# A one-layer hybrid encoder kernel: queries projected with the weights stationary and x^T moving, rotary embedding on rows packed through DRAM, pooling maps and one set of key transposes placed elsewhere

## The chip, the core and the metric

One Trainium2 chip, of which one core is used. The metric is the device time of one execution in microseconds (us), median of several runs. Engines are named as the profile names them: PE (TensorE, matmuls; PEld are its weight loads), DVE (VectorE), ACT (ScalarE), POOL (GpSimd) and SP (SyncE, which here only issues DMAs; ACT issues a few too). Each engine works through its own queue in order.

## The reference, cut to what is computed

```python
D_MODEL, SEQ, N_HEADS, D_LATENT = 1024, 2048, 8, 128      # one layer, batch 1
proj = x @ w_in        # columns: q 1024 | c_kv 128 | q_idx 512 | w_idx 8 | k_idx 64 | pool_in 512 | gates 2048
q = apply_partial_rope(q.reshape(B, S, N_HEADS, D_LATENT), cos_q, sin_q)   # first 32 of 128 dims: two halves of 16
k_lat = apply_partial_rope(c_kv, cos_q, sin_q)
q_idx, k_idx = ...     # rotated in the same way, 16 of 64 dims
attn = sparse_indexed_attention(q, k_lat, c_kv, q_idx, w_idx, k_idx)   # each query keeps its 256 best keys
attn = jnp.einsum('bshd,hde->bshe', attn, w_uv).reshape(B, S, ATTN_WIDTH)
branch_a = attn @ w_attn_branch
branch_b = multiscale_pool(pool_in, w_pool, pool_scale) @ w_pool_branch  # trailing means minus token, a 128x128 map per group
gate_a, gate_b = jnp.split(jax.nn.sigmoid(gate_logits), 2, axis=-1)
mixed = (gate_a * branch_a + gate_b * branch_b) @ w_out
x = layer_norm(ALPHA * x + mixed); x = layer_norm(ALPHA * x + conv_ffn(x))

def apply_partial_rope(x, cos, sin):     # half = 16 for q
    x1, x2 = x[..., :half], x[..., half:2 * half]
    return jnp.concatenate([x1 * cos - x2 * sin, x2 * cos + x1 * sin, x[..., 2 * half:]], axis=-1)
```

## The kernel before

Every float32 operand of a projection is split into a high and a low part (`split`, L312: on POOL in pieces of 256 columns, or on ACT for the high and DVE for the low part), and each product is three matmuls (`mm3`, L337). The 2048 tokens are worked in four groups of 512 (`G`), each of four row blocks of 128 (`RB`).

`run` (L1839) goes through these stages: for each group `proj_index` (indexer, keys and values; tokens in the rows of the result) and `finish_index` (rotary embedding of those rows); then for each group `proj_pool`, `proj_q` and `proj_gates`; then attention, the output projection and the feed-forward part. The steps that follow are in the second loop.

`proj_r` (L523) makes a product with tokens in rows: the stationary operand is a 128x128 piece of x^T, the moving one 256 columns of the weights. `proj_t` (L513) makes it transposed: the stationary operand is a 128x128 piece of the weights, the moving one 512 tokens of x^T. The pools and gates go by `proj_t`, the queries by `proj_r`. So `proj_q` (L648) computes, for four weight chunks of 256 columns (two heads), four row blocks of 24 matmuls of 256 columns each; ACT copies each result out; DVE rotates the rows (four products and two sums of 128x128 elements per chunk, `rope`, L534); and two chunks later `store_q` (L672) transposes them back on PE, 128x128 at a time (eight transposes per chunk, 32 per group), since attention wants q as (dim, head, token). ACT copies the transposed heads out and issues their store to `d_q`. `load_q` (L1064) fetches them, 128 tokens at a time, in attention.

Where `store_q` is called: from `proj_q` once more than two chunks are pending, and at the first two chunks of `proj_gates`. At the fourth gate chunk stand the four pooling maps (`pool_map`, L752; three matmuls each with `wpool`, their results taken out by ACT and DVE). The transposes of the last group's keys (`keys`, called through `done()`, L1869) stand after the second step of the first group's `proj_pool`.

What sets the order: the code is written as generators that yield between pieces of PE work. At each yield `turn` (L359) runs what was put off for some turns (`after`), issues the stores put off with `store` (SP, two turns later), and then, as a set of modelled clocks allows, takes steps from a background list: the indexer's scores (matmuls with `kst`) and a 32-step bisection for each query's 256th score (tiles `F`, `g`, `h`, `wd`, `wa`: counts on DVE and ACT over whole rows, each with a throw-away output from the pool of small tiles). That pool (`M`) has 8 buffers, the pool of large tiles (`T`) 42, and PSUM four banks of 512 columns (`PS1`) for the projections. Weights are fetched two chunks ahead and split one chunk ahead (`Weights.get`, L250), in group 0 from `w_in`, where the split parts are also stored (`wp`), and in later groups from those stored parts.

## Time and profile before

| | us |
|---|---|
| median of three runs | 3289.72 (3289.57 to 3299.82) |
| the profiled execution, its own time | 3292.94 |
| its span, first to last instruction | 3291.2 |
| PE busy in the span | 3157.8 (96%) |
| DVE, ACT, POOL busy | 2417.7 (73%), 1559.4 (47%), 1279.9 (39%) |
| mean granted clock of PE | 0.982 of 2.4 GHz |

In this trace the first loop ends at about 196 us with the first pooling matmuls; the keys' transposes of the last group begin at 201.8, group 0 of the second loop ends at 428.8, and the first matmul of attention starts at 1099.8. Nearly every operation is recorded by one helper and so has the line L153; rows are told apart by tiles and shapes. In tile names p is PSUM, b a large and m a small tile. A window of the trace gives, per engine, its busy time and in brackets the instructions in it, then PEclk, the granted clock as a share of 2.4 GHz, the DMA engines' busy share and GB/s.

### The profile page before, as it was taken

The numbers are of one execution on the slowest core, as the hardware profiler recorded it, in microseconds if no ns is written. First come the engines' busy times: TensorE is split into PE (matmuls) and PEld (weight loads), VectorE is DVE, ScalarE is ACT, GpSimd is POOL, SyncE is SP. The second block draws the span as 40 slices with busy tenths as digits, with TensorE's granted clock in tenths as the row PEclk, the third lists the DMA queues.
The fourth block names the chain that finished last, engine by engine and source line by source line (L and its number), as shares of the span: only waits on it lengthen the run. The fifth ranks groups of instructions, "written<-read, shape, count | busy, mean of one in ns | idle before, by whom it ended". The sixth has DMA issues, their size and how long they took to land. (4 is left out here: it accounts for less than half of the span.)

```text
span 3291.2 us, 46503 instructions
## 1 busy us (share of the span) xinstructions
PE 3157.8 (96%) x15918; PEld 2654.2 (81%) x15918; DVE 2417.7 (73%) x4271; ACT 1559.4 (47%) x2656; POOL 1279.9 (39%) x1314
## 2 busy tenths in 40 slices
PE   8988899999999899999999999999999999999998
PEld 8877688898898788788878877777778778888787
DVE  5588859986988777777766666666688865555797
ACT  3466537846777466666621133333343433222443
POOL 3139411020010688766641143443166511121673
PEclk9999899999999899999999999999999999999999
DMA  8457565653665444434464459899797665566984
GB/s 327 148 199 275 191 251 195 246 203 136 227 226 194 144 172 172 157 130 161 157 224 147 156 186 320 309 327 339 288 380 264 208 252 224 224 238 246 364 296 163
DMA packets 325675, 745.68 MB, mean 227 GB/s; under 512 B 30074, under 2 KB 115006, under 8 KB 325438
## 3 DMA queue, kind: packets, MB, share of 16 engines
q1 hardware_dynamic: 315646, 724.88, 61.5%
q10 hardware_dynamic: 9792, 17.83, 1.4%
q8 instruction: 126, 2.06, 0.3%
q14 instruction: 111, 0.91, 0.1%
HBM read 514.36 MB, written 228.23 MB: 226 GB/s over the span
## 5 line engine op out<-in xcount | busy, mean ns | idle before, releaser
L153 PE MATMUL p<-b,b 128*128 128x512 f32 (+3 forms) x12644 | 2783.7, 369 | 56.1 <-ACT b L153 24.4
L153 PEld LDWEIGHTS p<-b,b 128*128 128x128 f32 x12644 | 2175.7, 191 | 453.0 <-ACT b L153 25.0
L153 ACT ACTIVATE b<-p 128x512 fp32r<-128x512 f32 (+9 forms) x726 | 427.7, 612 | 653.6 <-PE p L153 627.0
L153 ACT ACTIVATE b<-b 128x1024 fp32r<-128x1024 f32 (+2 forms) x248 | 253.6, 1028 | 390.7 <-POOL b L153 136.4
L153 DVE TENSOR_TENSOR b<-b,b 128x1024 fp32r<-128x1024 f32 (+6 forms) x246 | 369.6, 1541 | 42.6 <-ACT b L153 39.8
L153 ACT ACTIVATE m<-b,F 128x1024 bf16<-128x1024 f32 (+3 forms) x352 | 345.8, 985 | 68.0 <-DVE F L153 43.8
L153 DVE TENSOR_SCALAR_CACHE_REDUCE m<-b,F 128x768 bf16<-128x768 f32 (+4 forms) x374 | 346.8, 949 | 11.8 <-DMA q<-m 9.9
L153 POOL TENSOR_TENSOR b<-b,b 128x256 fp32r<-128x256 f32 (+3 forms) x276 | 314.1, 1152 | 101.7 <-ACT b L153 84.9
L153 DVE TENSOR_TENSOR m<-m,p 128x512 f32<-128x512 f32 x176 | 120.3, 684 | 242.8 <-ACT b L153 182.6
L153 POOL TENSOR_TENSOR m<-b,b 128x512 f32<-128x512 f32 x99 | 140.2, 1425 | 337.4 <-issue 258.6
L153 DVE SCALAR_TENSOR_TENSOR b<-b,cw,b 128x1023 f32<-128x1023 f32 (+1 forms) x176 | 245.0, 1392 | 26.2 <-ACT b L153 25.1
L153 DVE TENSOR_TENSOR b<-p,b 128x512 fp32r<-128x512 f32 (+1 forms) x286 | 201.7, 714 | 72.3 <-ACT b L153 69.7
L153 POOL TENSOR_SCALAR b<-b 128x256 fp32r<-128x256 f32 (+3 forms) x216 | 125.8, 596 | 325.6 <-DMA b<-in_w_in_dram 122.8
L153 PE MATMUL p<-b 128*128 128x512 f32 x616 | 235.1, 393 | 5.8 <-ACT b L153 4.0
L153 POOL TENSOR_TENSOR b<-b,m 128x512 f32<-128x512 f32 x110 | 192.0, 1760 | 123.8 <-DMA m<-in_w_ffn_down_dram 74.0
L153 PE MATMUL p<-ident,b 128*128 128x128 f32 x1456 | 213.1, 274 | 24.8 <-ACT b L153 13.5
L153 DVE CUSTOM_DVE_ANT_0 b<-p,b 128x1024 f32<-128x1024 f32 (+7 forms) x192 | 174.2, 909 | 65.8 <-PE p L153 64.5
L153 PEld LDWEIGHTS p<-ident,b 128*128 128x128 f32 x1456 | 174.2, 141 | 58.7 <-ACT b L153 16.5
L153 ACT ACTIVATE b<-b,mx 128x1024 f32<-128x1024 f32 (+7 forms) x192 | 171.5, 896 | 69.7 <-DVE mx L153 63.7
L153 ACT ACTIVATE m<-p 128x512 f32<-128x512 f32 (+1 forms) x180 | 104.9, 594 | 193.6 <-PE p L153 178.9
L153 DVE SCALAR_TENSOR_TENSOR b<-b,ws,b 128x768 f32<-128x768 f32 (+5 forms) x154 | 159.8, 1065 | 40.6 <-ACT b L153 38.6
L153 PE MATMUL p<-kst,b 128*128 128x384 f32 (+3 forms) x656 | 150.6, 359 | 4.1 <-ACT b L153 2.6
(130 smaller groups left out, 2360.8 us busy)
## 6 DMA issues: line engine op xcount, KB each, us to landing
b<-uw SPq DMA_DIRECT2D x308, 512.0 KB, 6.5
b<-wp SPq DMA_DIRECT2D x192, 512.0 KB, 5.8
uw<-l SPq DMA_DIRECT2D x98, 512.0 KB, 3.0
b<-in_w_ffn_down_dram SPq DMA_DIRECT2D x154, 256.0 KB, 5.3
b<-h SPq DMA_DIRECT2D x154, 256.0 KB, 5.3
wp<-b SPq DMA_DIRECT2D x64, 512.0 KB, 5.2
uw<-b SPq DMA_DIRECT2D x56, 512.0 KB, 3.5
h<-m SPq DMA_DIRECT2D x110, 256.0 KB, 5.9
```

The lines of the kernel that those rows point to most:

```text
L153: return f(*args, **kw)
```

## The change

The queries go by `proj_t`: for each head one unit of 24 matmuls with 512 moving columns, whose result is already (dim, token). ACT copies it to a small tile `t` two turns later and stores dims 32 to 127 to `d_q`; SP stores the two halves of 16 rotary dims to `d_qx`, so that 8 heads x 16 dims fill 128 rows. At the second gate chunk these are loaded (`rope_load`), and during the third DVE rotates them with six operations of 128x512 (`rope_turn`) and stores them to `d_qr`; `load_q` fetches q in three pieces. The tables of cosines and sines come in the same packing: POOL widens them, PE transposes them (eight transposes per group) and ACT copies them out, in the first loop. `store_q` is gone. Of the splits that went to POOL, every fourth of all splits counted in the first two loops now goes to ACT and DVE. The four pooling maps stand between the units of the gates, one after each of units 4 to 7. The last keys' transposes stand four steps later.

```diff
+KEYS_AT = 5
+PM_AT = (4, 5, 6, 7)
...
     def split(self, hi, lo, src, pool=False):
-        if pool:
+        self.turns += 1
+        if pool and (not self.shared or self.turns % 4):
...
     def proj_index(self, g, done):
+            if c == 1:
+                self.rope_wide(g)
+            if c == 2:
+                self.rope_tables(g)
...
+    def rope_wide(self, g):
+        self.wide = []
+        for tab in (self.cos, self.sin):
+            t = self.M([P, RB, H, ROT])
+            self.nc.gpsimd.tensor_copy(t, tab[:, g * RB:(g + 1) * RB, None, :].to_broadcast([P, RB, H, ROT]))
+            self.wide.append(t)
+    def rope_tables(self, g):
+        nc = self.nc
+        for i, wide in enumerate(self.wide):
+            ps = self.PS1()
+            for rb in range(RB):
+                nc.tensor.transpose(ps[:, rb * P:(rb + 1) * P], wide[:, rb].rearrange("p h r -> p (h r)"), self.ident)
+            t = self.M([P, G])
+            nc.scalar.activation(t, ps, AF.Copy)
+            self.store(self.d_cs[g][:, i], t)
     def proj_q(self, g):
...
         for c in range(4):
             w = self.ab.get(base + c)
+            for i in range(2):
                 ps = self.PS1()
+                yield from self.proj_t(ps, w, i * P)
+                def keep(ps=ps, h=2 * c + i):
+                    t = self.M([P, G])
+                    nc.scalar.activation(t, ps, AF.Copy)
+                    nc.scalar.dma_start(self.d_q[g][2 * ROT:, h], t[2 * ROT:])
+                    for s in range(2):
+                        nc.sync.dma_start(self.d_qx[g][s][h * ROT:(h + 1) * ROT], t[s * ROT:(s + 1) * ROT])
+                self.after(DG, keep)
+                for _ in range(2):
                     self.lazy_step()
+                yield 5.2
+    def rope_load(self, g):
+        self.cs, self.qx = self.T([P, 2, G]), self.T([P, 2, G])
+        self.nc.sync.dma_start(self.cs, self.d_cs[g])
+        for s in range(2):
+            self.nc.sync.dma_start(self.qx[:, s], self.d_qx[g][s])
+    def rope_turn(self, g):
+        nc = self.nc
+        x, c, o = self.qx, self.cs, self.T([P, 2, G])
+        m = {}
+        def half(i, j, op):
+            def mul():
+                nc.vector.tensor_tensor(o[:, i], x[:, i], c[:, 0], op=OP.mult)
+            def cross():
+                m[i] = self.M([P, G])
+                nc.vector.tensor_tensor(m[i], x[:, j], c[:, 1], op=OP.mult)
+            def add():
+                nc.vector.tensor_tensor(o[:, i], o[:, i], m[i], op=op)
+                self.store(self.d_qr[g][i], o[:, i])
+            return [mul, cross, add]
+        return half(0, 1, OP.subtract) + half(1, 0, OP.add)
     def proj_gates(self, g):
...
-            if j == 3:
-                yield from self.pool_map(g)
-            if self.qpend and j < 2:
-                self.store_q()
+            if j == 1:
+                self.rope_load(g)
             while self.lazy or j and self.fins:
                 self.lazy_step()
+            if j == 2:
+                turning = self.rope_turn(g)
             for i in range(2):
                 ps = self.PS1()
-                yield from self.proj_t(ps, w, i * P)
+                for step in self.proj_t(ps, w, i * P):
+                    if j == 2:
+                        turning.pop(0)()
+                    yield step
...
-                yield 5.2
+                if 2 * j + i + 1 in PM_AT:
+                    yield 2.6
+                    self.pool_map(len(self.pm))
+                yield 2.6
...
     def load_q(self, b):
         q = self.T([P, H, P])
-        nc.sync.dma_start(q, self.d_q[g][:, :, rb * P:(rb + 1) * P])
+        cs = slice(rb * P, (rb + 1) * P)
+        nc.sync.dma_start(q[2 * ROT:], self.d_q[g][2 * ROT:, :, cs])
+        for s in range(2):
+            nc.sync.dma_start(q[s * ROT:(s + 1) * ROT], self.d_qr[g][s][:, cs].rearrange("(h r) c -> r h c", h=H))
...
             for i, step in enumerate(self.proj_pool(g)):
-                if i == 1 and g == 0:
+                if i == KEYS_AT and g == 0:
                     done()
```

Three places in the order of instructions. The first is PE in group 0, at the first pair of heads that `store_q` transposes. In the names p is a PSUM tile and b an SBUF tile, with the numbers of the program; `ident` is the identity of a transpose. Before:

```order
L153 MATMUL p_929_3797<-b_3420,b_2862 128x256
L153 MATMUL p_929_3797<-b_3420,b_2861 128x256
L153 MATMUL p_929_3797<-b_3421,b_2861 128x256
L153 MATMUL p_929_3797<-b_3420,b_2862 128x256
L153 MATMUL p_942_3850<-ident_84,b_3208 128x128 x4
L153 MATMUL p_944_3858<-ident_84,b_3208 128x128 x4
L153 MATMUL p_957_3895<-b_3629,b_2210 128x256
L153 MATMUL p_957_3895<-b_3630,b_2210 128x256
```

Now, between two units of the queries:

```order
L155 MATMUL p_830_3290<-b_2953,b_3132 128x512
L155 MATMUL p_830_3290<-b_2954,b_3132 128x512
L155 MATMUL p_830_3290<-b_2953,b_3133 128x512
L155 MATMUL p_853_3363<-b_2284,b_3122 128x512
L155 MATMUL p_853_3363<-b_2285,b_3122 128x512
L155 MATMUL p_853_3363<-b_2284,b_3123 128x512
```

The transposes are gone from PE's queue there, and one unit of 512 columns stands where two of 256 stood. Over the whole program PE has 15054 matmuls where it had 15918: 1536 of 256 columns are replaced by 768 of 512, 128 transposes are gone and 32 are added.

The second place is PE in group 0 at the pooling maps (tile `wpool`). Before, the four stand together between two units of the gates:

```order
L153 MATMUL p_1140_4540<-b_2861,b_4299 128x512
L153 MATMUL p_1168_4631<-b_3338,wpool_586 128x512 x3
L153 MATMUL p_1171_4641<-b_3516,wpool_586 128x512 x3
L153 MATMUL p_1178_4662<-b_3745,wpool_586 128x512 x3
L153 MATMUL p_1180_4669<-b_4032,wpool_586 128x512 x3
L153 MATMUL p_1184_4681<-b_2210,b_4459 128x512
```

Now the first of them, with a whole unit of 24 matmuls before it and one behind it:

```order
L155 MATMUL p_1098_4160<-b_2953,b_3927 128x512
L155 MATMUL p_1098_4160<-b_2954,b_3927 128x512
L155 MATMUL p_1098_4160<-b_2953,b_3928 128x512
L155 MATMUL p_1114_4221<-b_3347,wpool_606 128x512 x3
L155 MATMUL p_1128_4254<-b_2284,b_4069 128x512
L155 MATMUL p_1128_4254<-b_2285,b_4069 128x512
```

Each map has moved to a place of its own, 24 matmuls from the next.

The third place is SP in group 0's queries, between the stores of split weights (`wp`) and the fetches of later ones (`in_w_in_dram`). Before:

```order
L366 DMA wp_3432<-b_3194 128x1024
L366 DMA wp_3433<-b_3195 128x1024
L366 DMA wp_3649<-b_3410 128x1024
L212 DMA b_3625<-in_w_in_dram 128x4x256
L212 DMA b_3627<-in_w_in_dram 128x4x256
```

Now:

```order
L369 DMA wp_3288<-b_3132 128x1024
L369 DMA wp_3289<-b_3133 128x1024
L688 DMA qr_157<-m_3370 16x512
L688 DMA qr_158<-m_3370 16x512
L369 DMA wp_3457<-b_3272 128x1024
L369 DMA wp_3458<-b_3273 128x1024
L214 DMA b_3439<-in_w_in_dram 128x4x256
L214 DMA b_3441<-in_w_in_dram 128x4x256
```

Two stores of 16 rows from ACT's tile now stand in SP's queue for every head (64 in all), ahead of a later chunk's fetch; SP has 124 DMAs more.

## Rows read from the trace of the kernel before

**Rows 1.** The page's head, the busy time of each engine.

```profile
span 3291.2 us, 46503 instructions
PE 3157.8 (96%) x15918; PEld 2654.2 (81%) x15918; DVE 2417.7 (73%) x4271; ACT 1559.4 (47%) x2656; POOL 1279.9 (39%) x1314
```

**Rows 2.** Windows: group 0 of the second loop, the next part up to the end of group 1's queries, the rest of the second loop, and the start of attention.

```profile
201.80:428.80 227.00, 193.51 (x989) 164.62 (x988) 201.85 (x536) 128.47 (x250) 145.15 (x256) 0.90 0.69 245
428.80:560.00 131.20, 123.16 (x777) 110.45 (x776) 98.16 (x181) 78.81 (x141) 18.20 (x18) 0.97 0.50 186
560.00:1078.00 518.00, 515.52 (x2698) 444.46 (x2697) 441.33 (x1086) 366.65 (x673) 30.51 (x39) 1.00 0.59 211
1078.00:1131.00 53.00, 46.85 (x212) 38.23 (x211) 43.76 (x112) 22.84 (x59) 35.86 (x46) 0.84 0.45 143
```

**Rows 3.** PE's timeline in group 3, at the end of the queries and in the gates: start, duration and number of matmuls that follow each other in one shape.

```profile
971.24 1.04 PE L153 MATMUL p<-ident,b 128*128 128x128 f32 x8
972.04 11.75 PE L153 MATMUL p<-b,b 128*128 128x256 f32 x96
983.62 1.47 PE L153 MATMUL p<-ident,b 128*128 128x128 f32 x12
987.44 0.66 PE L153 MATMUL p<-ident,b 128*128 128x128 f32 x4 [2.35 <-ACT b L153]
...
1024.52 71.13 PE L153 MATMUL p<-b,b 128*128 128x512 f32 x313
```

**Rows 4.** The shapes on PE in group 0 (201.8 to 428.8), with the idle time before each and what ended it.

```profile
L153 PE MATMUL p<-b,b 128*128 128x512 f32 x553 | 132.4, 402 | 4.1 <-DVE b L153 3.4 <-ACT m L153 0.7
L153 PE MATMUL p<-b,b 128*128 128x256 f32 x384 | 49.8, 294 | 2.4 <-ACT b L153 2.4
L153 PE MATMUL p<-ident,b 128*128 128x128 f32 x32 | 5.3, 306 | 6.9 <-ACT b L153 6.9
L153 PE MATMUL p<-b,wpool 128*128 128x512 f32 x12 | 5.1, 550 | 9.8 <-ACT m L153 9.8
L153 PE MATMUL p<-ident,m 128*128 128x128 f32 x8 | 3.2, 412 | 10.2 <-DVE m L153 10.2
```

**Rows 5.** Windows inside group 0: the keys and the pools, the queries, the gates up to the maps, the maps.

```profile
201.80:232.90 31.10, 20.89 (x81) 15.89 (x80) 27.79 (x91) 16.53 (x31) 15.87 (x36) 0.78 0.64 227
232.90:295.40 62.50, 53.18 (x410) 52.03 (x408) 60.57 (x164) 43.64 (x93) 49.46 (x85) 0.93 0.66 229
295.40:332.30 36.90, 36.16 (x155) 29.61 (x154) 29.46 (x68) 21.18 (x40) 33.96 (x63) 0.94 0.95 349
332.30:350.60 18.30, 5.11 (x13) 2.51 (x12) 16.77 (x46) 13.77 (x28) 12.72 (x24) 0.65 0.76 232
```

**Rows 6.** The costliest small operations and the rotary operations on DVE in group 0: number, busy time, mean ns of one, idle time before.

```profile
L153 DVE SCALAR_TENSOR_TENSOR g<-wd,wa 128x4 f32<-128x4 f32 x32 | 16.7, 522 | 7.6 <-ACT m L153 6.9
L153 DVE TENSOR_SCALAR h<-g 128x4 int32<-128x4 f32 x32 | 10.8, 339 | 1.0
L153 DVE TENSOR_SCALAR h<-g 128x2 int32<-128x2 f32 x31 | 10.1, 325 | 1.0
L153 DVE SCALAR_TENSOR_TENSOR g<-wd,wa 128x2 f32<-128x2 f32 x31 | 9.2, 295 | 2.2 <-ACT m L153 1.8
L153 DVE SCALAR_TENSOR_TENSOR F<-h,F 128x4 int32<-128x4 int32 x31 | 8.7, 280 | 1.0
L153 DVE SCALAR_TENSOR_TENSOR F<-h,F 128x2 int32<-128x2 int32 x31 | 8.1, 261 | 1.0
L153 DVE TENSOR_TENSOR rope<-b,sin 128x128 f32<-128x128 f32 x8 | 4.5, 559 | 0.0
L153 DVE TENSOR_TENSOR rope<-b,cos 128x128 f32<-128x128 f32 x8 | 3.9, 492 | 0.0
L153 DVE TENSOR_TENSOR b<-rope,rope 128x128 f32<-128x128 f32 x8 | 3.7, 501 | 0.0
```

**Rows 7.** The same small operations on DVE from 570 to 680 us, a stretch of the second loop in which POOL is nearly idle.

```profile
L153 DVE TENSOR_SCALAR h<-g 128x2 int32<-128x2 f32 x46 | 7.8, 169 | 1.3
L153 DVE SCALAR_TENSOR_TENSOR g<-cd,ca 128x2 f32<-128x2 f32 x46 | 7.2, 157 | 4.6 <-ACT m L153 3.6
L153 DVE SCALAR_TENSOR_TENSOR F<-h,F 128x2 int32<-128x2 int32 x45 | 7.2, 160 | 1.4
```

**Rows 8.** The splits on POOL in group 0 (pieces of 256 columns, two operations each), and operations of the second loop (0 to 1131 us) on DVE that are like those that the change adds.

```profile
L153 POOL TENSOR_TENSOR b<-b,b 128x256 fp32r<-128x256 f32 x114 | 85.1, 767 | 0.0
L153 POOL TENSOR_SCALAR b<-b 128x256 fp32r<-128x256 f32 x114 | 50.3, 459 | 10.4 <-DMA b<-in_w_in_dram 6.7 <-DMA b<-in_w_pool_branch_dram 3.6
...
L153 DVE TENSOR_TENSOR b<-b,b 128x1024 fp32r<-128x1024 f32 x20 | 25.0, 1270 | 12.8 <-ACT b L153 12.3 <-DMA xT<-b 0.3
L153 DVE TENSOR_TENSOR b<-m,b 128x512 fp32r<-128x512 f32 x16 | 11.9, 745 | 0.7 <-ACT b L153 0.7
```

**Rows 9.** Waits of PE in group 1's queries and gates (530 to 572 us): in total, times, longest.

```profile
PE p L153 <- ACT b L153: 4.6, 2, 2.7
```

**Rows 10.** Waits for DMAs from 201.8 to 1131 us that end an idle time of DVE or ACT, and the two longest of SP's own queue from 428.8 to 1131 us.

```profile
DVE m L153 <- DMA q<-m: 9.9, 4, 3.1
ACT m L153 <- DMA q<-m: 6.4, 3, 3.4
DVE m L153 <- DMA gm<-m: 1.1, 1, 1.1
ACT m L153 <- DMA gm<-m: 1.0, 1, 1.0
...
SPq L220 <- DVE b L153: 131.2, 19, 29.4
SPq L220 <- PE p L153: 106.5, 39, 23.8
```

More of the change, by code (lines that the diff above doesn't have):

```diff
@@ L451, in setup @@
         self.d_q = [self.DT([P, H, G], name="q") for _ in range(NG)]
+        self.d_qx, self.d_qr = ([[self.DT([P, G], name="qr") for _ in range(2)] for _ in range(NG)] for _ in range(2))
+        self.d_cs = [self.DT([P, 2, G], name="cs") for _ in range(NG)]
         self.d_gm = [self.DT([P, DC, 2, G], name="gm") for _ in range(NG)]
@@ L650, in proj_q @@
         base = g * self.nab + 2
-        bs = slice(g * RB, (g + 1) * RB)
         for c in range(4):
             w = self.ab.get(base + c)
-            rows = self.T([P, RB, 256])
-            for rb in range(RB):
+            for i in range(2):
                 ps = self.PS1()
-                yield from self.proj_r(ps[:, :256], w, rb, 256)
-                self.after(DQ, lambda rb=rb, ps=ps, rows=rows:
-                           nc.scalar.activation(rows[:, rb], ps[:, :256], AF.Copy))
-                if rb:
-                    self.lazy_step()
-                yield 2.6
-            self.flush()
-            v = rows.rearrange("p b (h d) -> p b h d", d=DL)
-            cs, sn = (t[:, bs, None, :].to_broadcast([P, RB, 2, ROT]) for t in (self.cos, self.sin))
-            halves = (v[:, :, :, 0:16], v[:, :, :, 16:32])
-            self.rope(halves, halves, cs, sn, [P, RB, 2, ROT])
-            self.qpend.append((g, c, rows))
-            if len(self.qpend) > 2:
-                self.store_q()
@@ L672, in store_q @@
-    def store_q(self):
-        g, c, rows = self.qpend.pop(0)
-        for i in range(2):
-            ps = self.PS1()
-            for rb in range(RB):
-                self.nc.tensor.transpose(ps[:, rb * P:(rb + 1) * P], rows[:, rb, i * DL:(i + 1) * DL], self.ident)
-            t = self.M([P, G])
-            self.nc.scalar.activation(t, ps, AF.Copy)
-            self.nc.scalar.dma_start(self.d_q[g][:, 2 * c + i], t)
+                yield from self.proj_t(ps, w, i * P)
[5 more added lines that the diff above has]
+                        nc.sync.dma_start(self.d_qx[g][s][h * ROT:(h + 1) * ROT], t[s * ROT:(s + 1) * ROT])
@@ L750, in lazy_step, with pool_map @@
             self.lazy.pop(0)()
[L752 removed]
+    def pool_map(self, k):
         nc = self.nc
[L754 to L764 removed]
+        t = self.pooled[k]
+        ps = self.PS1()
+        self.mm3(ps, self.wpool[:, 0, k], self.wpool[:, 1, k], t[:, 0], t[:, 1], True, True)
+        o = self.T([P, 2, G], F32R)
+        sc = self.pscale[:, k:k + 1]
+        nc.scalar.activation(o[:, 0], ps, AF.Identity, scale=sc)
+        nc.vector.scalar_tensor_tensor(o[:, 1], ps, sc, o[:, 0].bitcast(F32), op0=OP.mult, op1=OP.subtract)
+        self.pm.append(o)
     def proj_gates(self, g):
```

23 lines of the change are left out of this document (7 added, 16 removed).

## The prediction

> **What bounds the kernel now.** I read the page's head first: PE is busy for 96% of the span, no other engine for over 73% [rows 1]. So the end is set by PE's work plus the time in which PE waits or runs at the lower of its two clocks. The change touches the second loop (196 to 1100 us), so I next read that loop in windows [rows 2]. From 560 to 1078 us PE is busy for 515.5 of 518 us at full clock (2.4 GHz): there a matmul less is time less. Group 0 is different: in 227.0 us PE's granted clock is 0.90 on average, and DVE is busy for 201.9 us. The matmuls' own need there follows from the counts [rows 4] and the spacing at full clock [rows 3]. Spacing is read from starts, since durations overlap: 96 matmuls of 256 columns go from 972.04 to 983.62, 120.6 ns each; 313 of 512 columns take 71.13 us, 227 ns each; eight transposes go from 971.24 to 972.04, 100 ns each. So 565 x 0.227 + 384 x 0.1206 + 40 x 0.1 = 178.6 us, and group 0 loses 48.4 us. The idle times in rows 4 say where: 10.2 us at the keys' transposes (waiting for DVE's rotations), 9.8 at the pooling maps, 9.3 in the queries and at their transposes, 4.1 behind the maps; the rest is time at the lower clock, which follows the waits (0.78 around the keys, 0.65 at the maps [rows 5]).
>
> **What the change removes and adds on PE.** Two matmuls of 256 columns become one of 512: 2 x 120.6 - 227 = 14.2 ns less for each of 768, 10.9 us in all, 2.7 per group. The columns streamed stay the same, so this is what a matmul costs beside its columns. The 128 transposes go: 128 x 0.1 = 12.8 us, 3.2 per group. The 32 of the tables come: 3.2 us in the first loop, on PE, which has little else to wait for them; bounds 0 (they fall into waits that are there anyhow) and 10 (the keys' eight transposes idled 10.2 us behind DVE [rows 4], these follow POOL copies issued a chunk earlier, so I stay with their own time). In groups 1 to 3 the gain is 3 x 5.9 = 17.7 us, since PE is the limit there.
>
> The Trainium skill, TensorE: Matmul & The Clock Gate, section Back-to-back issue gap, gives a warm matmul N/2.4 + 2.5 ns; by it a pair would save only 2.6 ns and all pairs 2.0 us, so that the sum would be 8.9 us smaller. The trace disagrees on the narrow shape (120.6 ns against 109.2), and the trace decides.
>
> **Waits that go with the transposes.** In groups 1 to 3 PE's waits at `store_q` are 4.6 us [rows 9] and 2.35 us [rows 3]. Both wait for ACT's copies of the query rows; a transposed unit needs no such copy before PE goes on, only a free PSUM bank of four. The lower clock costs 0.03 x 131.2 = 3.9 us between 428.8 and 560 [rows 2]; I give half of it to the first of these waits. Together 9 us, between 5 and 11.
>
> **Group 0.** Here PE's need falls to 172.7 us (757 x 0.227 and the keys' eight transposes), but DVE has to get through its rows too, and PE waits for DVE by way of PSUM, the rotations and the split weights. So I size this term by DVE. Its 201.9 us change as follows. The rotations of 128x128 go: 4.5 + 3.9 + 3.7 = 12.1 us [rows 6]; six of 128x512 come, at 0.745 [rows 8] 4.5 us. Nine of the splits in this stretch move from POOL to ACT and DVE (counted in the order; three more are outside): 9 x 1.27 = 11.4 us on DVE [rows 8], and 36 pieces x (0.767 + 0.459) = 44.1 us less on POOL, 30% of its 145.2. That matters to DVE: its small operations take 0.522, 0.339, 0.325, 0.295, 0.280 and 0.261 us in group 0 [rows 6], and 0.157 to 0.169 where POOL is nearly idle [rows 7]. The excess, 32 x 0.365 + 32 x 0.170 + 31 x 0.156 + 31 x 0.138 + 31 x 0.120 + 31 x 0.101, is 33 us; if 30% of it goes with POOL's work, 10 us. So DVE needs 201.9 - 12.1 + 4.5 + 11.4 - 10 = 195.7 us. Up to the maps' end it idled 148.8 - 134.6 = 14.2 us [rows 5]; with that kept the stretch takes 209.9, 17 us less than 227. Bounds: 6 if DVE keeps all its idle time of 25.2 us, or 7 if POOL's lighter load relieves it of nothing; 54 if DVE's backlog does not hold PE at all (227 - 172.7). The waits at the keys and maps have no terms of their own: PE reaches the keys two pooling pairs (24 x 0.227 = 5.4 us) later and each map has its own place, but what PE gains there it can keep only as far as DVE follows.
>
> A rule of the Trainium skill speaks against the moved splits: SBUF — State Buffer, section Who interferes with whom, says that a DVE instruction with two SBUF inputs and a GpSimd instruction that reads SBUF lock each other out for a whole instruction. By it each moved split could stand behind one POOL piece, up to 9 x 0.767 = 6.9 us, and this term would be 10 rather than 17. The rule fits the slow small operations of rows 6; the 20 like splits of rows 8 show no such delay in their mean.
>
> **What costs nothing, and what covers it.** POOL's eight wide copies stand in the first loop. The rotation's load and its six DVE steps lie two gate chunks behind the queries, and `d_qr` is read only in attention; if that cover went, nothing before attention would wait for it. ACT copies as many 512-column results per group as before at the transposes, and 16 of 256 less. Each head's two SP stores wait for ACT's copy, and the fetches of later weights stand behind them in SP's queue; SP already waits there for DVE and PE, 131 and 107 us in all from 428.8 to 1131 [rows 10], without PE waiting for a fetch, since these run two chunks ahead.
>
> **Sum.** 17 + 17.7 - 3.2 + 9 = 40.5 us. Against the profiled execution's 3292.9 us that is 3252.4; the median of the runs is 3.2 us below it, so 3249.
>
> **Rivals.** (1) DVE takes it back. Group 0 gives its lower bound, 6, and the transposes' waits return as waits for a PSUM bank: 6 + 17.7 - 3.2 = 20.5, 3269 us. For it: DVE is busy for 89% of group 0 and gets nine splits more. Against: POOL's load falls by more. (2) Group 0 gives back nearly all: the keys, the maps and the transposes were the only places where PE stood, and the lower clock followed them. Then 54 + 17.7 - 3.2 + 9 = 77.5, 3212 us. For it: without them PE has nothing at hand to wait for in rows 4 but 6.5 us. Against: DVE's need. (3) Slower. A head's copy now sits in one of the eight small tiles until two SP stores have landed, and these stand in SP's queue behind stores and fetches that wait up to 29.4 us at a time [rows 10]; the counts of the bisection take two such tiles per step, so DVE and ACT stop when the ring comes round. In groups 0 and 1 (16 heads) DVE has no room to make that up. At 3.4 us per head, the longest such wait behind `q` today [rows 10], 54 us, 3303 us; it decides from (40.5 + 9.9) / 16 = 3.2 us per head. Against: the gates' second halves are stored by SP from such tiles today, and cost DVE and ACT 1.1 and 1.0 us in all. (4) The 14.2 ns of a pair are not the narrow shape's own but something that stays, and pairs save nothing: 40.5 - 10.9, 3260 us; against it stand the equal starts of rows 3. The rule of the Trainium skill on the issue gap, above, would come near to this case. (5) The order's change moves the waits elsewhere and PE's saving is lost in new ones, around 3285.
>
> **How the numbers follow.** About 0.3%, 10 us, is what a measurement of this kernel can tell from no change. I give the forecast 0.59, (1) 0.18, (2) 0.12, (3) 0.05, (4) 0.03, (5) 0.03. The likeliest gives the time, 3249. The range 3220 to 3272 holds the forecast with its bounds, (1), (4) and the near part of (2); it leaves out (3), (5) and what of (2) lies below, some 0.15. Faster by over 0.3%: 0.59 + 0.18 + 0.12 + 0.03, less a little for what I overlooked, 0.90; within 0.3%: 0.04; slower: 0.06.
>
> **What would show it.** In the profile after: 768 matmuls of 512 columns more and the units at 227 ns; groups 1 to 3 of the second loop each about 6 us shorter, with PE busy throughout; group 0 near 210 us with a granted clock above 0.90, its DVE time near 196 us and the `g` and `h` operations shorter; no wait of PE at `wpool` of several us. It would be wrong if DVE's or ACT's idle time before DMAs of `qr` came to tens of us, if the maps' waits turned up at the gates' PSUM tiles, or if the start of attention (clock 0.84 [rows 2]) lost more than now.

## The result and the profile after

| | before | after |
|---|---|---|
| median, us | 3293.33 of 4 runs (3289.57 to 3299.82) | 3263.89 of 4 runs (3258.59 to 3270.37) |
| ratio, 95% interval | | 0.9909 (0.9883 to 0.9936) |
| span of the profiled execution | 3291.2 | 3268.6 |

The change saves 29.4 us by the medians and 22.6 between the two profiled spans; the profiled execution after is the slowest of its four. The page's head of the kernel after answers to [rows 1]:

```profile
span 3268.6 us, 44761 instructions
PE 3143.0 (96%) x15054; PEld 2605.0 (80%) x15054; DVE 2403.2 (74%) x4211; ACT 1554.2 (48%) x2612; POOL 1223.3 (37%) x1226
```

To see where it went, cut both traces at the same places of the program: the first pooling matmul, the first of each later group, the end of the second loop (the last matmul of the gates), the 56th score tile of attention, the 120th, and the matmul from which both programs run the same 7566 matmuls to the end (1539.4 and 1513.5 us). Six of these windows of the kernel before (columns as in [rows 2]): the first loop, group 0, group 2, group 3, the start of attention (up to the 56th tile), and the stretch from the 120th tile to the common point.

```profile
0.00:196.33 196.33, 179.63 (x1386) 173.69 (x1387) 114.42 (x276) 86.49 (x174) 45.17 (x114) 1.00 0.62 226
196.33:428.85 232.52, 199.03 (x1015) 169.12 (x1014) 207.25 (x550) 131.55 (x261) 150.62 (x265) 0.90 0.68 240
...
673.02:914.93 241.91, 241.91 (x1293) 210.19 (x1292) 198.97 (x384) 153.81 (x244) 17.45 (x20) 1.00 0.53 191
914.93:1095.03 180.10, 177.75 (x980) 155.13 (x979) 158.17 (x389) 121.55 (x225) 25.50 (x34) 1.00 0.60 209
1095.03:1230.13 135.10, 120.19 (x666) 100.99 (x665) 102.38 (x252) 82.06 (x181) 109.06 (x107) 0.92 0.41 139
...
1402.62:1539.41 136.79, 136.75 (x783) 116.04 (x782) 100.97 (x198) 88.44 (x168) 83.64 (x85) 1.00 0.41 145
```

The same windows of the kernel after, with group 1 (244.2 us before) between:

```profile
0.00:204.76 204.76, 185.41 (x1418) 178.80 (x1419) 118.86 (x279) 91.22 (x182) 39.80 (x112) 0.98 0.63 225
204.76:411.53 206.77, 189.27 (x791) 151.68 (x790) 190.85 (x534) 135.09 (x256) 117.75 (x195) 0.95 0.79 283
411.53:647.71 236.18, 229.35 (x1054) 188.94 (x1052) 192.65 (x480) 162.00 (x320) 17.11 (x22) 0.99 0.64 231
647.71:884.71 237.00, 236.99 (x1069) 195.78 (x1068) 197.12 (x368) 146.91 (x227) 13.78 (x20) 1.00 0.56 198
884.71:1056.03 171.32, 171.32 (x756) 141.72 (x755) 158.74 (x381) 125.36 (x225) 24.68 (x24) 1.00 0.65 233
1056.03:1199.29 143.26, 123.45 (x667) 104.22 (x665) 110.80 (x268) 83.08 (x183) 106.61 (x101) 0.89 0.43 137
...
1371.65:1513.52 141.87, 138.44 (x782) 116.97 (x781) 98.94 (x196) 87.34 (x167) 82.61 (x84) 0.99 0.41 140
```

The lengths give the ledger: first loop +8.4, group 0 -25.7, group 1 -8.0, group 2 -4.9, group 3 -8.8, attention's start +8.2, on to the 120th tile -0.1, on to the common point +5.1, the rest +3.3; in all -22.5. Group 0's clock rose from 0.90 to 0.95 and its DVE time fell by 16.4 us. Four items have the wrong sign. The rest is scatter of this one execution (+0.6 in the next profile of the same kernel); the other three are the first loop, attention's start and the stretch before the common point.

**The first loop.** SP's timeline of the kernel before, in the last group of that loop (start, us, line): the stores of rotated rows, then those of x^T, then the fetch of the first pooling weights.

```profile
127.87 4.24 SPq L366 DMA_DIRECT2D qi<-b  x2
132.34 6.65 SPq L366 DMA_DIRECT2D xT<-b  x6
139.08 2.53 SPq L212 DMA_DIRECT2D b<-in_w_in_dram  x2
```

And after, with the tables' stores (`cs`) ahead and the rows' stores strung out:

```profile
133.58 1.24 SPq L369 DMA_DIRECT2D cs<-m  x2
135.54 0.32 SPq L369 DMA_DIRECT2D qi<-b  x1
...
144.11 0.32 SPq L369 DMA_DIRECT2D qi<-b  x1
...
146.52 1.85 SPq L214 DMA_DIRECT2D b<-in_w_in_dram  x2
```

The fetch leaves 7.4 us later. One of its two splits had moved to ACT, and the waits after, from 140 to 158 us, read (who waited for what: us in total, times, longest):

```profile
PE p L155 <- ACT b L155: 6.4, 2, 6.2
ACT b L155 <- DMA b<-in_w_in_dram: 6.0, 1, 6.0
```

Over the whole loop PE's waits grow by only 2.4 us (16.5 to 18.9), since shorter ones go. The rest of the 8.4 is the tables' transposes, 3.2, and the lower clock behind the long wait: 0.81 from 147 to 165 us, where the loop before ran at 1.00 throughout; that is about 3.4 us.

**Attention's start.** The selection of the last blocks ends with a scan on DVE. After, two scans fall between attention's units (DVE's timeline; the first attention matmul is at 1057.1); before, they stood at 1099.5 and 1146.5, with that matmul at 1099.8.

```profile
1115.07 5.13 DVE L155 TENSOR_TENSOR_SCAN b<-b 128x1920 f16<-128x1920 f16 x1
...
1154.51 5.38 DVE L155 TENSOR_TENSOR_SCAN b<-b 128x2048 f16<-128x2048 f16 x1
```

PE stands 4.5 and 4.3 us behind them, and its waits from 1056 to 1199 us are mostly for DVE:

```profile
PE p L155 <- DVE b L155: 14.5, 4, 5.2
PE p L155 <- DVE mx L155: 3.8, 5, 1.7
```

The longest, 5.2 us, stands behind no scan: it ends with a split on DVE at attention's first units, before which DVE waited 3.8 us for POOL. In all PE waits 19.8 us in this stretch where it waited 14.7, and its clock is 0.89 where it was 0.92.

### The profile page after: what moved, and what is told of

It is laid out like the page before. It is cut to its first block, busy times and chain, and to the rows that moved or that the text cites. A ratio compares the mean times of both kernels' runs of the same rounds, so it can differ in the third digit from the quotient of the medians.

```text
span 3268.6 us, 44761 instructions
## 1 busy us (share of the span) xinstructions
PE 3143.0 (96%) x15054; PEld 2605.0 (80%) x15054; DVE 2403.2 (74%) x4211; ACT 1554.2 (48%) x2612; POOL 1223.3 (37%) x1226
## 4 chain that ended last, share of the span: by engine, by line
PE 74%; DVE 10%; DMA 5%; issue 5%; POOL 4%; ACT 2%; SPq 0%; POOLq 0%; DVEq 0%; ACTq 0%
PE p L155 74%; DVE b L155 5%; DVE m L155 3%; POOL b L155 2%; ACT b L155 2%; DMA b<-h 1%; POOL l L155 1%; DMA b<-in_w_in_dram 1%; POOL m L155 1%; DVE h L155 1%; DVE g L155 0%; ACT m L155 0%; DMA gm<-m 0%; DVE F L155 0%; DMA b<-wp 0%
## 5 line engine op out<-in xcount | busy, mean ns | idle before, releaser
L155 PEld LDWEIGHTS p<-b,b 128*128 128x128 f32 x11876 | 2132.6, 191 | 518.3 <-DVE b L155 41.6
L155 ACT ACTIVATE b<-p 128x512 fp32r<-128x512 f32 (+9 forms) x662 | 404.1, 635 | 616.3 <-PE p L155 570.5
L155 ACT ACTIVATE b<-b 128x1024 fp32r<-128x1024 f32 (+2 forms) x260 | 266.3, 1029 | 403.6 <-POOL b L155 135.7
L155 DVE TENSOR_TENSOR b<-b,b 128x1024 fp32r<-128x1024 f32 (+6 forms) x266 | 387.4, 1492 | 50.2 <-ACT b L155 44.0
L155 POOL TENSOR_TENSOR b<-b,b 128x256 fp32r<-128x256 f32 (+3 forms) x228 | 284.7, 1262 | 102.6 <-ACT b L155 86.7
L155 PE MATMUL p<-b 128*128 128x512 f32 x616 | 236.3, 396 | 6.1 <-ACT b L155 3.8
L155 POOL TENSOR_TENSOR b<-b,m 128x512 f32<-128x512 f32 x110 | 185.3, 1698 | 131.1 <-DMA m<-in_w_ffn_down_dram 71.2
L155 POOL TENSOR_SCALAR b<-b 128x256 fp32r<-128x256 f32 (+3 forms) x168 | 100.9, 614 | 333.6 <-ACT b L155 110.3
L155 PE MATMUL p<-ident,b 128*128 128x128 f32 x1328 | 197.4, 276 | 5.2 <-DMA b<-x 2.9
L155 PEld LDWEIGHTS p<-ident,b 128*128 128x128 f32 x1328 | 162.0, 142 | 37.5 <-DVE b L155 3.7
```

The costliest lines, as they stand in the source:

```text
L155: return f(*args, **kw)
```

## The experiments

Each was timed in five rounds; the kernel before had medians of 3292 to 3296 us beside them. The table has each median, the ratio to before with its interval, and the lengths of the ledger's stretches in the profiled execution (group 3 and attention's start together). The intervals of most neighbours in it overlap; what single runs show rests on the stretches, each from one profile.

| kernel | median | ratio (95% interval) | first loop | group 0 | group 1 | group 2 | group 3 to 56th tile | 120th tile to common point |
|---|---|---|---|---|---|---|---|---|
| before | 3293.3 | | 196.3 | 232.5 | 244.2 | 241.9 | 315.2 | 136.8 |
| after | 3263.9 | 0.9909 (0.9883-0.9936) | 204.8 | 206.8 | 236.2 | 237.0 | 314.6 | 141.9 |
| again | 3265.1 | 0.9909 (0.9895-0.9923) | 205.9 | 205.0 | 235.9 | 236.9 | 314.6 | 143.1 |
| first_on_pool | 3265.8 | 0.9908 (0.9893-0.9924) | 205.2 | 206.9 | 236.3 | 237.0 | 314.4 | 143.1 |
| rate_077 | 3275.7 | 0.9943 (0.9929-0.9956) | 204.9 | 226.3 | 233.6 | 236.8 | 305.6 | 141.8 |
| rate_080 | 3270.2 | 0.9928 (0.9914-0.9942) | 206.4 | 229.7 | 220.6 | 247.3 | 298.6 | 143.1 |
| tables_early | 3259.6 | 0.9887 (0.9871-0.9902) | 201.4 | 204.1 | 236.6 | 236.9 | 315.3 | 142.2 |
| late_082 | 3267.4 | 0.9908 (0.9892-0.9923) | 204.4 | 206.0 | 236.2 | 238.2 | 312.2 | 141.9 |
| no_sharing | 3270.8 | 0.9921 (0.9903-0.9938) | 205.0 | 208.5 | 241.9 | 237.0 | 312.4 | 141.9 |
| maps_together | 3270.1 | 0.9919 (0.9904-0.9934) | 203.7 | 210.5 | 238.0 | 237.2 | 315.7 | 142.8 |
| one_fetch | 3255.5 | 0.9882 (0.9863-0.9901) | 203.9 | 207.8 | 235.7 | 237.1 | 311.5 | 136.7 |
| keys_at_1 | 3272.0 | 0.9928 (0.9915-0.9942) | 204.6 | 211.9 | 237.2 | 236.9 | 315.7 | 141.6 |
| rotation_on_pool | 3264.8 | 0.9906 (0.9890-0.9921) | 200.4 | 205.3 | 236.8 | 240.9 | 315.2 | 143.7 |
| early_and_whole | 3250.9 | 0.9866 (0.9843-0.9889) | 201.7 | 204.2 | 235.6 | 236.9 | 313.2 | 136.7 |

**again**: the changed kernel, unaltered.

> The changed kernel once more, unaltered, as a yardstick. Theory: what it lost beside its gains is a property of its order and returns in every execution: the first loop ends near 204.8 us (first pooling matmul), with one wait of PE of about 6 us for ACT shortly before 155 us, and the two longest scans of the selection (128x1920 and 128x2048 on DVE, 5.1 and 5.4 us) fall behind the first matmul of attention with a wait of PE of over 4 us at each. Rival: these losses are scatter of one execution; then the first loop ends near 199.5 (196.3 and the tables' 3.2) or the waits at the scans are under 2 us. Time by both 3264, give or take 6.

The table's stretches return within 2 us, the two scans at the same distances from attention's first matmul. So the ledger up to the common point belongs to the program, not to one execution.

**first_on_pool**, from the kernel after:

```diff
-                    self.ab.split(0)
+                    self.alone = True
+                    self.ab.split(0)
+                    self.alone = False
...
-        if pool and (not self.shared or self.turns % 4):
+        if pool and (not self.shared or self.alone or self.turns % 4):
```

> The changed kernel, but the two splits of the first pooling weights, in the last group of the first loop, stay on POOL (the count of turns goes on, so every other split stays where it was). Theory: of these two the change gave one to ACT, whose queue then stood 6.0 us for that weight's fetch while PE waited 6.2 us for ACT's copies; with it back on POOL the first loop ends near 199, 5.7 us earlier than 204.8, and the whole takes 3264 - 6 = 3258. Rival: the 8.5 us are the price of the widened tables on POOL and of their 32 transposes on PE; then the first loop still ends at 203.5 to 205.5 and the time stays at 3264.

The theory fell: the wait at 149 us is gone and the loop is as long. Waits of this run from 157 to 170 us:

```profile
ACT b L155 <- POOL b L155: 7.7, 1, 7.7
PE p L155 <- ACT b L155: 5.9, 1, 5.9
```

Now ACT waits for a large tile that POOL's late split still holds. Whoever splits, the weights come late; the place to look is the fetch.

**rate_077** and **rate_080**:

```diff
-RATE = 0.75
+RATE = 0.77
```

> The changed kernel with the rate at which background steps are let in per us of modelled PE time at 0.77 instead of 0.75. Theory: the change took 20.8 us of PE's work out of the second loop; at 0.75 that is 15.6 us of selection work that no longer fits before attention, and its two longest scans moved behind attention's start, where PE waits for DVE. At 0.77 both scans stand where they stood before the change (by PE's own work 1.3 us ahead of attention's first matmul and 32.6 us behind it, against 1.2 and 30.8), so the stretch from the first attention matmul over 457 us shrinks by 8 to 13 us and the whole takes 3251 to 3257. Rival: attention loses because the queries are now fetched in three pieces, two of them of 16-row blocks from the rotated copies; then the stretch keeps its length within 2 us, scans or not, and the time is 3262 to 3266.

> The same rate at 0.80, so that both longest scans come ahead of attention's first matmul by PE's own work (36.6 and 14.6 us ahead). Theory: no wait of PE behind a scan in attention at all, so that attention's first 457 us come out 3 to 6 us shorter still than at 0.77, at 438 to 443 us; against that DVE has more to do per us in the second loop, busy there for 86 to 89% as it is, and may hold PE in group 0 or 1 by up to 6 us. Time 3245 to 3257. Rival (the fetch in pieces): attention keeps 455 to 459 us and the time is 3262 to 3270.

Attention's part is as expected: group 3 to the 56th tile is 9 and 16 us shorter, with the scans earlier, so the scans are what PE waits for there and the rival is refuted for this stretch. But the time is 5 to 11 us worse than again's, since group 0 takes 20 and 23 us more: more selection steps stand there, and PE's waits in group 0 double (17.1 us in the kernel after, 34.7 in rate_077, of which 28.7 for DVE). These are rate_077's group 0 and its stretch from group 3 on:

```profile
204.90:431.20 226.30, 191.63 (x789) 153.25 (x790) 199.03 (x534) 133.33 (x252) 115.56 (x194) 0.91 0.75 261
901.60:1207.20 305.60, 289.74 (x1422) 243.20 (x1421) 258.67 (x624) 201.68 (x393) 118.91 (x124) 0.97 0.56 191
```

**late_082**: the higher rate only where PE loses little.

```diff
+LATE = 0.82
...
-        self.credit = min(self.credit + RATE * (pe - self.seen), CAP)
+        self.credit = min(self.credit + (LATE if self.late_on else RATE) * (pe - self.seen), CAP)
...
         for g in range(NG):
+            self.late_on = g > 1
```

> The changed kernel with the rate at which background steps are let in at 0.75 in groups 0 and 1 and at 0.82 in groups 2 and 3 only. In the two runs with a higher rate throughout, attention's first units were 14 and 22 us shorter and group 0 20 to 23 us longer. Theory: PE has room for DVE's and ACT's steps in groups 2 and 3, where it lost 4.0 and 0.9 us to waits, and none in group 0. Then attention's stretch from its first matmul over 56 score tiles is 122 to 130 us (142.2 at 0.75), groups 0 and 1 stay at 205 to 207 and 236, groups 2 and 3 grow by 0 to 5 us, and the whole takes 3248 to 3256. Rival: selection's work costs PE the same wherever it stands, because DVE is busy for 83 and 93% of groups 2 and 3; then these grow by 10 us or more and the time is 3262 to 3268.

The theory fell. Groups 0 to 2 stay (238.2 in group 2), and the whole stays too. From attention's first matmul to the 56th tile it takes 130.1 us instead of 142.2, but group 3 takes 182.1 up to that matmul instead of 172.4, the growth that the rival named. One scan is now ahead of attention's first matmul; the other meets its first units, with a single wait of 8.9 us. PE's waits from 1054 to 1100 us:

```profile
PE p L156 <- DVE mx L156: 12.7, 3, 8.9
```

A rate with both scans ahead of attention and group 0 left alone was not run, so whether the 8.2 us of attention's start can be had stays open.

**tables_early**:

```diff
-            if c == 1:
-                self.rope_wide(g)
-            if c == 2:
-                self.rope_tables(g)
+            for k, do in TABLES.get((g, c), ()):
+                getattr(self, do)(k)
...
+W, X = "rope_wide", "rope_tables"
+TABLES = {(0, 1): [(0, W)], (0, 2): [(0, X), (1, W)], (1, 0): [(1, X), (2, W)], (1, 1): [(2, X), (3, W)], (1, 2): [(3, X)]}
```

> The changed kernel, but all tables of cosines and sines are widened and transposed in groups 0 and 1 of the first loop instead of one group's in each of the four (the same eight copies and 32 transposes). Theory: the loss in the first loop (it ends at 205 to 206 us instead of 196.3, where the transposes' own time is 3.2 to 3.5) is a ring: in group 2 the widened and the transposed tables sit in four of the eight small tiles, so that DVE's rotations of that group's rows, which want two of them, come 20 us of PE's work later (they are rotated behind the last unit instead of between the units), their stores stand before the first pooling weights' fetch in SP's queue, and the fetch goes out at 146.5 us instead of 139.1, with 6 us of PE's waiting behind it. With the tables out of the way of that group the fetch goes out near 142.5 and the first loop ends at 199 to 201. Time 3264 - 5 = 3259. Rival: the transposes and POOL's copies cost it wherever they stand, and the first loop still ends at 204 to 206.

With the same eight copies and 32 transposes the loop ends at 201.4, 3.4 to 4.5 us earlier (forecast 199 to 201), and the median falls by 4.3 to 5.5 us, with overlapping intervals. The fetch goes out at 144.42 (forecast 142.5), and PE's waits from 125 to 170 us, 6.4 for ACT in the kernel after, are

```profile
PE p L157 <- DVE b L157: 2.9, 3, 1.4
PE p L157 <- ACT b L157: 0.2, 1, 0.2
```

So 3.4 to 4.5 us of the loss were the tables' place. That it acts through the ring of eight small tiles is read from the order of instructions; a run with more small tiles was not made. Of the 5.1 us left against before, 3.2 are the transposes' own time, and the lower clock is most of the rest, 1.8 us in this window of the run:

```profile
117.00:128.00 11.00, 10.86 (x69) 10.29 (x68) 9.34 (x31) 7.32 (x16) 0.00 (x0) 0.84 0.37 131
```

**no_sharing**:

```diff
-        if pool and (not self.shared or self.turns % 4):
+        if pool:
```

> The changed kernel without its shared splits: all splits that went to POOL before stay on POOL. By the prediction's sizing of group 0 by DVE: nine splits of 1.36 us less on DVE are 12.2, and the operation on g, which fell from 522 to 297 ns with POOL's load, goes back by 7.2, so that DVE needs 5 less and group 0 takes 200 to 207 us against 206.8. Rival: POOL, with 36 more pieces of two operations (44 us), becomes late with the weights, and group 0 takes 212 us or more, with waits of PE for POOL; then most of the group's gain of 26 us is owed to the moved splits. The first loop by both within 2 us of 205. Time 3259 to 3264, by the rival 3270 and more.

Group 0's length is 208.5, between the two; the time, 3270.8, is the rival's. Its window:

```profile
205.00:413.50 208.50, 191.28 (x791) 150.63 (x790) 194.30 (x525) 127.51 (x247) 151.04 (x266) 0.95 0.76 273
```

DVE has nine splits fewer and is busy for 3.4 us more than in the kernel after, with POOL at 151 us instead of 118. The nine splits cost DVE in the kernel after:

```profile
L155 DVE TENSOR_TENSOR b<-b,b 128x1024 fp32r<-128x1024 f32 x9 | 12.2, 1358 | 0.0
```

So POOL's larger load costs DVE 12.2 + 3.4 = 15.6 us. The six narrow operations of [rows 6] (`g`, `h` and `F` of four and of two) take 9.9 of that, and all of them lengthen; `h` of four in the kernel after and here:

```profile
L155 DVE TENSOR_SCALAR h<-g 128x4 int32<-128x4 f32 x32 | 10.8, 338 | 0.9
L155 DVE TENSOR_SCALAR h<-g 128x4 int32<-128x4 f32 x32 | 12.2, 382 | 1.0
```

The median is 6 to 7 us worse; group 1 takes 5.7 of that. PE's waits for POOL in group 0 are 4.4 us where they were 0.9, the rival's sign at a small size.

**maps_together** and **keys_at_1**, each one move of the change undone:

```diff
-PM_AT = (4, 5, 6, 7)
+PM_AT = ()
...
+            if j == 3:
+                for k in range(4):
+                    self.pool_map(k)
+                    yield 0.7
```

> The changed kernel with the four pooling maps together again ahead of the fourth gate chunk. By the prediction's sizing by DVE the maps have no term of their own: group 0 stays at 205 to 209 us, since what PE waits at the maps it would wait elsewhere. Rival: the waits at the maps are PE's own loss, as in the kernel before (18.3 us in that place for 2.7 us of matmuls); then group 0 takes 216 to 222 us. In group 1 the waits of 4.0 and 2.1 us behind single maps go, and come back there by at most as much as before (none of over 1 us stood at the maps of that group).

```diff
-KEYS_AT = 5
+KEYS_AT = 1
```

> The changed kernel with the last keys' transposes back at the second step of the first pooling chunk. By the prediction's sizing by DVE that place has no term of its own and group 0 takes 204 to 209 us (205.0 to 206.8). Rival: what PE idled there before the change, 10.2 us and the lower clock of 0.78 with it, was PE's own loss and comes back; then group 0 takes 214 to 222 us and the whole 3272 to 3280.

Both fall between theory and rival: group 0 takes 4 to 6 and 5 to 7 us more, the medians are 5 to 6 and 7 to 8 us worse, with overlapping intervals. In group 1 PE's waits at single maps, 3.9 and 1.9 us, come back as 5.7 and 1.7 with the maps together, and the group is no shorter (238.0 against 236).

**one_fetch**: from the kernel after,

```diff
-                    nc.scalar.dma_start(self.d_q[g][2 * ROT:, h], t[2 * ROT:])
+                    nc.scalar.dma_start(self.d_q[g][:, h], t)
...
-        nc.sync.dma_start(q[2 * ROT:], self.d_q[g][2 * ROT:, :, cs])
-        for s in range(2):
-            nc.sync.dma_start(q[s * ROT:(s + 1) * ROT], self.d_qr[g][s][:, cs].rearrange("(h r) c -> r h c", h=H))
+        nc.sync.dma_start(q, self.d_q[g][:, :, cs])
```

> The changed kernel, but each head's whole 128 dims are stored to one place and attention fetches them in one piece; the rotation is still computed and stored, and not read, so attention works on queries that are not rotated. Theory: the three-piece fetch has no part in what is lost behind the second loop (5 us of waits more from group 3 to the 56th score tile, 5 to 6 more between the 120th and 1513 us); then these stretches stay within 2 us, at 314.6 and 142 to 143 us, and the time is 3262 to 3266. Rival: the pieces of 16 rows come late or crowd the queues; then the two stretches lose 5 us of waits each and the time is 3253 to 3258.

The rival is right for the second stretch: 136.7 us, the length of before. In the kernel after, PE's only wait from 1372 to 1513 us is

```profile
PE p L155 <- ACT b L155: 3.4, 1, 3.4
```

where ACT waits 3.2 us for POOL's split of the next block's queries; with one fetch PE has next to no wait in that stretch (0.1 us). Three kernels with one fetch have 136.7 to 136.8 there, eleven with three have 141.6 to 143.7. POOL's timelines show why its split comes later: its instructions stand in another order. In the kernel after, the split of a feed-forward weight (`l`) stands ahead of another split of 128x512 and waits for that weight's fetch; the two begin at

```profile
1458.33 0.62 POOL L155 TENSOR_SCALAR l<-b 128x512 fp32r<-128x512 f32 x1 [9.79 <-DMA b<-in_w_ffn_up_dram]
1458.92 0.63 POOL L155 TENSOR_SCALAR b<-b 128x512 fp32r<-128x512 f32 x1
```

and with one fetch

```profile
1456.04 0.62 POOL L155 TENSOR_SCALAR b<-b 128x512 fp32r<-128x512 f32 x1 [6.94 <-ACT b L155]
1458.01 0.61 POOL L155 TENSOR_SCALAR l<-b 128x512 fp32r<-128x512 f32 x1
```

All eleven with three fetches have the first order and a wait of 9.5 to 10.8 us there, and POOL's split of the next queries begins 108.0 to 109.3 us into the stretch; the three with one have the second order, and it begins at 106.0. PE then waits 3.3 to 4.4 us in the eleven and at most 0.1 in the three; the rest of the loss is lower clock. So the traces put the loss on the order on POOL; no run changed that order alone, and what decides it was not tested. The start of attention gains 3.1 us, less than the rival's 5, and the stretch between, from the 56th to the 120th tile, is 3.4 us longer than after and 5.9 longer than again.

**rotation_on_pool**: tables_early, and

```diff
+        e = nc.gpsimd if g else nc.vector
...
-                nc.vector.tensor_tensor(o[:, i], x[:, i], c[:, 0], op=OP.mult)
+                e.tensor_tensor(o[:, i], x[:, i], c[:, 0], op=OP.mult)
```

(so for all three forms of operation).

> The version with the early tables (3259.6), and the six rotations of 128x512 go to POOL in groups 1 to 3, where it is busy for 17 of 237 us; DVE gets rid of 18 x 0.685 = 12.3 us. In every version so far the waits of PE from group 0 to the 56th score tile add up to 88 to 99 us, wherever the selection's steps and the maps stand. Theory: DVE's work as a whole sets these waits in groups 1 to 3 and at the start of attention, so that a good part of the 12.3 us comes back: 4 to 10 us, and the time is 3250 to 3256. Rival: the waits are single collisions of order (a map behind a count, a copy behind a buffer), which less work on DVE doesn't remove; then the time stays at 3257 to 3262.

Groups 1 to 3 and attention's start are no shorter (group 2 is 4.0 longer), and the median is 5 us above that of tables_early, with overlapping intervals, and above the rival's range too. But the run does not test the theory, since DVE's busy time did not fall. Groups 1 to 3 in tables_early and here:

```profile
405.50:1050.60 645.10, 638.56 (x2877) 527.42 (x2875) 549.06 (x1224) 433.37 (x770) 63.52 (x70) 0.99 0.61 219
405.70:1055.10 649.40, 639.23 (x2877) 527.87 (x2875) 549.49 (x1206) 434.05 (x770) 86.98 (x87) 0.99 0.60 217
```

DVE has 18 operations fewer, 12.1 us of them, and is as busy as before: its other operations lengthened while POOL had 23.5 us more to do (`h` of two from 183 to 207 ns, 128 of them). Whether less work on DVE would shorten these groups stays open.

**early_and_whole**: tables_early with the rotated rows stored to the queries' own place and one fetch.

```diff
-        self.d_q = [self.DT([P, H, G], name="q") for _ in range(NG)]
+        self.d_q = [self.DT([H, P, G], name="q") for _ in range(NG)]
...
-                self.store(self.d_qr[g][i], o[:, i])
+                self.store(self.d_q[g][:, i * ROT:(i + 1) * ROT], o[:, i])
...
+        nc.sync.dma_start(q, self.d_q[g].rearrange("h d c -> d h c")[:, :, cs])
```

> The early tables (3259.6), and the rotated rows are stored back into the queries' own place, which now lies as (head, dim, token), so that attention fetches each block's queries in one piece, rotated. Theory: the two causes found, the ring of small tiles in the first loop and the fetch in three pieces, add up: the first loop ends at 200 to 202 us, the stretch from the 120th score tile to the common tail takes 136 to 138 us with 8 us of waits, as in the kernel before and with one fetch (142 to 143 and 13 to 14 in every run with three), POOL's waits for the feed-forward weights in attention come to 6 to 9 us instead of 18, and the whole takes 3249 to 3255. Rival: what one fetch saved came from not reading the rotated copies at all, and with the rotated rows written in pieces of 16 into the same place the time stays at 3258 to 3261.

Both repairs hold: 3250.9 us, 42.9 below before in the same rounds and 13 to 14 below the change. The interval of again lies above this one's; that of the change's first measurement overlaps it slightly (0.9883 against 0.9889). POOL's waits for the feed-forward weights (`l`) from 1200 us to the common point are 8.6 us, against 17.2 in the kernel after, as expected. Its first loop and its stretch up to the common point:

```profile
0.00:201.70 201.70, 185.05 (x1419) 178.42 (x1420) 118.39 (x279) 91.81 (x183) 42.39 (x110) 0.99 0.64 230
...
1360.00:1496.70 136.70, 136.65 (x782) 115.98 (x782) 99.76 (x196) 88.71 (x168) 85.46 (x86) 1.00 0.41 145
```

## Why the prediction was right, and where its terms were off

The direction and the range held: 40.5 us were forecast, 29.4 measured (22.6 between the profiled spans). That the sum came this near is in part luck. By the ledger group 0 gave 8.7 us more than its term, while groups 1 to 3 gave 5.0 less, the tables cost 5.2 more, and attention's start and the stretch before the common point lost 8.2 and 5.1 that no term held. By its terms:

**Pairs and transposes, 17.7 in groups 1 to 3.** Right in kind. Group 2, where PE never stood, is 4.9 us shorter of 5.9. (In the sum the pairs stand with 8.2 us only, 2.7 in each of groups 1 to 3, since group 0 is sized by DVE. If a pair saved 2.6 ns or nothing, the sum would therefore be 6.7 or 8.2 smaller, not 8.9 or 10.9, and rival (4) would come to 3257.) A long run of units after shows the spacing taken from [rows 3]; PE's timeline in group 3: 67.26 us for 296, 227 ns each.

```profile
904.66 67.26 PE L155 MATMUL p<-b,b 128*128 128x512 f32 x296
```

**Group 0, 17.** It gave 25.7 (27.5 in again), between the forecast and rival (2). DVE's time fell by 16.4 us (in windows 5 us wider) instead of 6.2: of the narrow operations `g` of four fell from 522 to 297 ns, while `h` of four stayed (339 to 338), though [rows 6, 7] had put both down to POOL. Between before and after much else in the order differs; no_sharing changes only where the splits are made, and by it the six narrow groups cost 9.9 us, as the 10 taken has it, with `g` of four at 368 ns and `h` at 382. The 5.7 us that POOL's load costs other operations had no term; nor does POOL's load explain most of the fall of `g`. The step that fell is that keys and maps have no terms of their own: undone alone they cost 5 to 7 and 4 to 6 us, though far less than the 10 us of idle time each showed in [rows 4]. With the sharing's 1.7 to 3.5 that is about half of the gain, if the three add up; the rest was not taken apart further.

**The moved splits.** The nine took 1358 ns, 88 more than the 1270 of [rows 8], 0.8 us together, where a whole POOL piece behind each would be 6.9. The Trainium skill, SBUF — State Buffer, section Who interferes with whom, has a DVE instruction with two SBUF inputs contend with a reading GpSimd; the runs agree that DVE is slower beside a busier POOL, by 15.6 us over the group (`h`, which reads one tile, lengthened too), but moving splits away from POOL relieved DVE more than it cost. No run here shows whether POOL is slowed in turn.

**Waits that go with the transposes, 9.** This term was sized too high. By the ledger, groups 1 to 3 gained 8.0 + 4.9 + 8.8 = 21.7 us where 26.7 were due; if pairs and transposes gave their 17.7, 4.0 are left for this term, below its bound of 5. Group 3 gave what was forecast for it, 5.9 and the wait of 2.35. In group 1 the 4.6 us of [rows 9] left, and these came at single maps (waits from 545 to 580 us, after):

```profile
PE p L155 <- ACT m L155: 3.9, 1, 3.9
PE p L155 <- DVE b L155: 1.9, 1, 1.9
```

**Attention's start, not priced.** It lost 8.2 us, 5.1 of waiting and about 3 at the lower clock, as the prediction's last sentence had named as a danger without a price. Background steps are let in by PE's work as the code models it; by that model 20.8 us less of it at a rate of 0.75 are 15.6 us of selection that no longer fit ahead of attention, and the scans moved into it. The two rate runs show this part (PE's waits there fall from 19.8 to 15.9 and 8.8 us); that it can be won back on the whole they don't show.

**Tables, 3.2 (0 to 10).** They cost 8.4 to 9.6, within the bounds for another reason than the one given. By the order of instructions it is rival (3)'s ring of eight small tiles at another place: the widened tables hold tiles that the rotations of keys want, their stores string out on SP, and the next fetch waits behind. tables_early shows that the tables' place costs 3.4 to 4.5 of it; the ring itself was argued, not tested. Most of what is left beyond their own time is lower clock (1.8 us in that run). At the queries the ring cost little: the waits of 9.9 and 6.4 us in [rows 10] are gone, and what DVE and ACT wait for DMAs of the queries from 204 to 1056 us after is only

```profile
ACT m L155 <- DMA b<-qr: 5.8, 1, 5.8
```

**Attention's fetch, not priced.** The prediction spoke of the rotation's cover before attention and passed over the fetch in three pieces. With it the stretch before the common point takes 5.1 to 6.3 us more, as one_fetch and early_and_whole show; the traces put it on the order on POOL.

Of the rivals, (1) needed a gain of 6 us in group 0, and (4) one of 3.2 in group 2 against 5.9 by the forecast, where 4.9 were measured; (2) would have had group 0 at twice its gain. (5) was partly so: part of what PE saved came back as waits elsewhere, 9 to 11 us of it in the two places that the last kernel mends.

## What to carry to other kernels

Price what a change does outside the stage it is made for: the buffers that its new temporaries hold, the fetches that stand behind its stores, and each consumer of a layout that it splits. When work is let in by another engine's progress, shortening that engine moves the work, and its longest piece must be looked for where it lands. An idle time in front of a step need not come back when the step is moved: here 10 us of idle time brought 4 to 7. Where an edit costs more than its own work, compare the order of instructions on each engine before and after, and where work is taken off an engine, check that its busy time fell.

## What the runs showed that was not expected

Six rotations per group on the nearly idle POOL instead of the busy DVE freed no time on DVE: 12.1 us of operations went, and its busy time over groups 1 to 3 stayed at 549 us, since other operations lengthened beside the busier POOL. And a stretch of 137 us before the common point held its length to 0.1 us in the three kernels that fetch each block's queries in one piece, and lost 5 to 7 us in all eleven that add two fetches of 64 KB per block. No engine waits there for one of the two; in all eleven two splits stand in the other order on POOL.
